# Last head pair of a FoX/RWKV-7 layer: its third block turned by VectorE and transfers, its fourth by TensorE

## The chip, the core and the metric

The kernel runs on one core of one Trainium2 chip. The core has TensorE (PE, matrix multiply, results in PSUM), VectorE (DVE), ScalarE (ACT), GpSimd (POOL) and SyncE (SP), whose queue issues nearly all transfers of this kernel; 16 DMA engines carry them. The metric is device time in microseconds (us) of one execution, as a median of several.

## The reference, cut to what matters

One layer for 256 frames and a width of 4096, all in float32. An input projection makes the columns of 16 attention heads (q, k, v of 128 columns each), of 32 RWKV-7 heads (r, k, v of 64 columns each) and of a gate z. Attention and RWKV results are gated by silu(z), joined, projected by `w_out`, and normalised with the residual.

```python
proj = jnp.einsum('bsd,dc->bsc', x, w_in)
fox_out = _fox_attention(fq, fk, fv, log_f)            # 16 heads of 128
y = _rwkv7_scan(rh, decay, kh, vh, -kk, kk * ah)       # 32 heads of 64
...
h = jnp.concatenate([fox_out, rwkv_out], axis=-1) * jax.nn.silu(z.astype(f32))
out = jnp.einsum('bsc,cd->bsd', h.astype(x.dtype), w_out)
x = _layernorm(ALPHA * x.astype(f32) + out.astype(f32), ln_gain, ln_bias, LN_EPS)
```

## The kernel before

**Tiling.** The projection is done in 8 pairs (`n` = 0 to 7, `G // 2` of them) of 4 blocks (`b` = 0 to 3) of 512 columns each. A block is 16 weight pieces `q` of 512 KB; each piece is split by ACT and DVE into a high and a low part (`w_qh`, `w_ql`; lines 141 and 142), and three matmuls per step (lines 147 to 149) give nearly float32 precision. After the 8 pairs comes the output projection over 8 blocks of 512 columns, with pieces `wo_q` and the same split (lines 882 to 884).

**Order of the work.** PE runs the projection's matmuls without a break, and everything else is done beside them. `block` calls `slot()` after every six matmuls (one k for both halves of the frames, or two k for one half), 32 times a block; in the first two blocks of the output projection (pieces 0 to 13) there is one slot per k. At a slot each generator in `sides` is advanced to its next `yield`; `wait(n)` is n slots. So slots fix the order in which instructions are written down. A planner in the framework then orders each engine's instructions by the time at which it reckons that their inputs are ready, so an instruction may move ahead of earlier written ones; `issue` (line 281) pins a transfer behind the one written before it on SP's queue. On the chip each engine and SP's queue work through the order they were given, and wait where an input is late.

**The blocks of a pair.** Block 0 holds RWKV r and k, block 1 RWKV v and attention v, block 2 the columns q, k, z of attention head 2n and z of RWKV (`fq`, `fk`, `zf`, `zr`), block 3 the same for head 2n+1. The results have frames on partitions; attention and gate want columns on partitions, so blocks 0, 2 and 3 are turned by `unload` (line 798), which starts two slots (`LAG`) after its block's end; block 2's waits in addition until the RWKV work of the pair before is done.

There are two ways to turn a block. In the general one (lines 809 to 815 and 843 to 847) DVE transposes both halves of `bk` in 32 x 32 squares (line 811), two slots later `turn` writes them in four transfers of 128 KB to a DRAM tile `bt`, two per slot, and four more transfers of 128 KB read `fq`, `fk`, `zf` and `zr` back from it in the wanted order, in rows of 32 elements. In the other (lines 832 to 841) PE transposes eight 128 x 128 tiles of `bk` against the identity `ident` into two PSUM tiles `tr`, and ACT copies them out. `last` (line 806) decides: in the kernel before, blocks 2 and 3 of pair 7 go by PE and all others by DVE and transfers.

**After the turn.** ACT scales `fq` (line 848), `fox(i, ...)` is started as a side (line 849), and the gate's tanh and product follow (`silu2`, line 367). `fox` multiplies q and k after 4 slots (`fsp`, lines 745 and 746), forms the softmax on DVE and ACT (lines 751 to 755), transposes it on DVE (line 757), copies it to `pT` (line 761), and multiplies it with v (`fop`, lines 766 and 767) 12 slots after `fsp`. `gate` (line 373) forms `h` and its two parts `hl`, and three slots later stores them in DRAM (`hd`, line 386) where the index k is under 29. Head 14 has k = 28 and is stored; head 15 (k = 30) and the RWKV halves 29 and 31 go straight into their tiles. `unload` of block 3 waits until `fox` of head 14 is through (line 828).

**What runs at the same time.** In block 3 of pair 7 the tiles of x come free step by step, and `get_h` (line 854) loads the stored `hd` of 256 KB each into them, 29 loads for the output projection, on SP's queue between the weight loads (line 218). RWKV of pair 7 solves its triangular systems on DVE meanwhile (lines 601 and 604), writes the result to `td` and reads it back as `T` (lines 611 and 613), turns v by transfers (`vt`, `vv`), and ends in the first blocks of the output projection. Weight loads have four buffers, the high parts four and the low parts three.

Of the kernel before, what the change touches and what calls it, by code (L numbers as in the profile page):

```python
# [21 lines left out]
G = 16  # L22
# [62 lines left out]
def layer(ctx: ExitStack, tc: tile.TileContext, xt, xtok, w_main, w_lora, w_first, muv, w_o, up, par, mulora, fbias, lng, lnb, cst, out):  # L85
# [9 lines left out]
    def pst(name):  # L95
        return ps.tile([P, 512], F32, tag="ps", name=name)
# [93 lines left out]
    def wait(n):  # L190
        for _ in range(n):
            yield

    def side(gen):
        sides.append(gen)
# [72 lines left out]
    def t256(tag, name, bufs=1):  # L268
        return rp.tile([P, S], F32, tag=tag, name=name, bufs=bufs)
# [10 lines left out]
    def issue(out, src):  # L280
        tc.keep_in_program_order(nc.sync.dma_start(out=out, in_=src))

    def turn(src, name, each=2):
        _, m, cols = src.shape
        d = dram.tile([cols // B, B, m, 4, B], F32, tag=f"dt{m}_{cols}", name=name, bufs=2)
        s = src.rearrange("p m (q t) -> p m q t", t=B)
        for a in range(4):
            issue(d[:, :, :, a, :].rearrange("q i m t -> i m q t"), s[B * a : B * (a + 1)])
            if a % each == each - 1:
                yield  # L290
        return d

    def shifted(p, n, i):
        r = t256(f"s{n}", f"s{n}_{i}", 2)
        lerp(p, prm[:, 7 + n, i : i + 1], omm[:, n, i : i + 1], r)
        return r
# [70 lines left out]
    def silu2(z, key):  # L367
        th = t256("zt", key + "t")
        nc.scalar.activation(th, z, AF.Tanh, scale=0.5)
        nc.vector.scalar_tensor_tensor(z, th, 1.0, z, ALU.add, ALU.mult)  # L370
        szs[key] = z
# [419 lines left out]
    def turned_back(d):  # L791
        return d.rearrange("(u b) i m a t -> u (b i) (m a t)", b=4).rearrange("u p s -> p u s")
# [5 lines left out]
    def unload(n, b, bk, vt):  # L798
        yield from wait(LAG)
        if b == 0:  # L800
            while n and 2 * n - 1 not in prepared:
                yield
        elif b == 2:
            while n and n - 1 not in done:
                yield
        last = n == G // 2 - 1 and b > 1
        if b == 3 and not last:
            yield from wait(BEHIND)
        if not last:
            for m in range(2):  # L810
                nc.vector.transpose(bk[:, m, :], bk[:, m, :])
            yield from wait(2)
            d = yield from turn(bk, f"bt{n}_{b}")
            unloading.clear()
            yield
        if b == 0:
            for u in range(2):
                i = 2 * n + u
                while n and n - 1 not in bonned:
                    yield  # L820
                raw = rp.tile([P, 2, S], F32, tag="s2", name=f"raw{i}")
                issue(raw, turned_back(d[8 * u : 8 * u + 8]))
                yield from wait(LAND)
                for j in range(2):
                    rk[i, j] = shifted(raw[:, j, :], j, i)
            return
        i = 2 * n + b - 2
        while i and i - 1 not in foxed:
            yield
        fq, fk = t256("fq", f"fq{i}"), t256("fk", f"fk{i}")  # L830
        zf, zr = t256("szf", f"zf{i}"), t256("szr", f"zr{i}", 2)
        if last:
            for h, pair in enumerate(((fq, fk), (zf, zr))):
                tr = pst(f"tr{h}")
                for t in range(2):
                    for m in range(2):
                        nc.tensor.transpose(tr[:, t * S + m * P : t * S + (m + 1) * P], bk[:, m, (2 * h + t) * P : (2 * h + t + 1) * P], ident)
                for t in range(2):
                    nc.scalar.copy(pair[t], tr[:, t * S : (t + 1) * S])
                yield  # L840
            unloading.clear()
        else:
            for j, t in enumerate((fq, fk, zf, zr)):
                issue(t, d[4 * j : 4 * j + 4].rearrange("b i m a t -> (b i) (m a t)"))
                if j % 2:
                    yield
            yield from wait(LAND - 1)
        nc.scalar.mul(fq, fq, FOX_SCALE)
        side(fox(i, fq, fk, vt))
        yield  # L850
        silu2(zf, f"f{i}")
        silu2(zr, f"r{i}")
# [62 lines left out]
    for n in range(G // 2):  # L915
        for b in range(4):
            acc = block(n, b)
            while unloading or b == 2 and n not in turned:
                slot()
            bk = rp.tile([P, 2, OB], F32, tag="bk", name=f"bk{n}_{b}") if n or b else bk_0  # L920
            for m in range(2):
                if b == 1:
                    nc.scalar.copy(bk[:, m, : 2 * P], acc[m][:, : 2 * P])
                elif not n and not b:
                    nc.scalar.copy(bk[:, m, P:], acc[m][:, :LB])
                else:
                    nc.scalar.copy(bk[:, m, :], acc[m])
            if b == 0:
                muvs[n] = rp.tile([P, 2 * P], F32, tag="prod", name=f"muv{n}")
                nc.sync.dma_start(out=muvs[n], in_=muv[n : n + 1, :].to_broadcast([P, 2 * P]))  # L930
            if b == 1:
                vd = vds[n % 2]
                bks[n] = bk[:, :, : 2 * P]
                nc.sync.dma_start(out=vd[1:].rearrange("(m p) c -> p m c", m=2), in_=bk[:, :, : 2 * P])
                vs_[n] = rp.tile([P, 2, 2 * P], F32, tag="vs", name=f"vs{n}")
                nc.sync.dma_start(out=vs_[n], in_=vd[:S].rearrange("(m p) c -> p m c", m=2))
                while n and 2 * n - 1 not in foxed:
                    slot()
                vt = rp.tile([P, 2, 2 * P], F32, tag="vt", name=f"vt{n}")
                for m in range(2):  # L940
                    nc.scalar.copy(vt[:, m, :], acc[m][:, 2 * P :])
            if b != 1:
                unloading.append(n)
                side(unload(n, b, bk, vt))
# [57 lines left out]
    def moments(m):  # L1002
        mv = rpool.tile([P, 2], F32, name=f"mv{m}")
        sd = rpool.tile([P, 1], F32, name=f"sd{m}")
        rs = rpool.tile([P, 1], F32, name=f"rs{m}")
        s2 = rpool.tile([P, 1], F32, name=f"s2{m}")
        zh = rpool.tile([P, 1], F32R, name=f"zh{m}")
        z = factors(m, "d")
        nc.gpsimd.memset(z[:, 3:5], 1.0)
        za = factors(m, "a") if m else None  # L1010
        add(m, NB - 1)
        nc.vector.bn_aggr(mv, sums if m else st[m].rearrange("p b s -> p (b s)"))
        mean = mv[:, 0:1]
        nc.scalar.activation(sd, mv[:, 1:2], AF.Sqrt, bias=lneps)
        nc.vector.reciprocal(rs, sd)
        nc.vector.tensor_tensor(s2, mean, rs, ALU.mult)
        nc.vector.tensor_copy(zh, s2)
        nc.vector.tensor_copy(z[:, 0:3:2], zh.bitcast(F32).to_broadcast([P, 2]))
        last = nc.vector.tensor_tensor(z[:, 1:2], s2, zh.bitcast(F32), ALU.subtract)
        s2s.append(s2)  # L1020
        if m:
            for n, (v, at) in enumerate(((mean, (slice(0, 3, 2), slice(1, 2))), (sd, (slice(3, 5), slice(5, 6))))):
                h = rpool.tile([P, 1], F32R, name=f"zah{n}")
                nc.scalar.copy(h, v)
                nc.scalar.copy(za[:, at[0]], h.bitcast(F32).to_broadcast([P, 2]))
                nc.scalar.activation(za[:, at[1]], h.bitcast(F32), AF.Identity, scale=-1.0, bias=v)
        rss.append(rs)
        return z, za, last.ins
# [18 lines left out]
    z0, _, last = moments(0)  # L1047
# [18 lines left out]
    z1, za, last = moments(1)  # L1066
# [7 lines left out]
    for n in range(HALVED):  # L1074
        b = HALVED + n
# [62 lines left out]
```

## Time and profile before

| | us |
|---|---|
| median of 3 runs | 1917.26 (1916.16 to 1917.36) |
| the profiled execution's own time | 1917.13 |
| its span in the profile | 1915.3 |
| PE busy | 1903.0 (99%) |
| PEld (weight loads into PE) busy | 1584.8 (83%) |
| DVE busy | 1398.3 (73%) |
| ACT busy | 985.9 (51%) |
| POOL busy | 261.5 (14%) |

1917.13 - 1915.3 = 1.8 us of the execution lie outside the span. Times below are in us from the span's start. "PE" rows are matmuls; a matmul's length overlaps that of its neighbours, so their pace is read from start to start. The DMA column of a table by windows is the mean busy share of the 16 DMA engines. The granted TensorE clock is 0.999 of full speed.

### The profile page before, as it was taken

Reading aid. Unit: us, or ns where it says so; the run is one execution under the profiler, and the core shown is the slowest. Engines: PE = TensorE matmul, PEld = TensorE weight load, DVE = VectorE, ACT = ScalarE, POOL = GpSimd, SP = SyncE. Lnnn points to the kernel's source line nnn. Section 1 sums busy time; section 2 is a strip of 40 time slices with the busy share of each in tenths; the row PEclk is TensorE's granted clock in tenths of the full one; section 3 lists DMA queues with packets and bytes.
Section 4 is the critical chain, followed back from the end, with each engine's and each line's share of the span. In section 5 each row is a group of like instructions: output and inputs, shape, how many; then the busy total and the mean of one; then the engine's idle time right before and its main releaser. Section 6 shows DMA issues by size and latency. Waiting matters only on the chain.

```text
span 1915.3 us, 27998 instructions
## 1 busy us (share of the span) xinstructions
PE 1903.0 (99%) x9784; PEld 1584.8 (83%) x9784; DVE 1398.3 (73%) x2359; ACT 985.9 (51%) x1543; POOL 261.5 (14%) x463
## 2 busy tenths in 40 slices
PE   9999999999999999999999999999999999999998
PEld 9878888888888888888888888888888878888886
DVE  6677868786877687768776877787778865765555
ACT  6554565455545654465446554645464554444332
POOL 0022102110211021102200220022002201000000
PEclk9999999999999999999999999999999999999999
DMA  9578767876787677767876687668767976876664
GB/s 338 152 232 230 205 198 235 229 216 190 228 232 220 189 228 224 230 191 217 233 227 193 208 242 226 194 208 246 215 196 207 300 255 199 271 222 202 183 203 170
DMA packets 269682, 420.58 MB, mean 220 GB/s; under 512 B 142370, under 2 KB 169396, under 8 KB 269540
## 3 DMA queue, kind: packets, MB, share of 16 engines
q1 hardware_dynamic: 269108, 418.10, 72.8%
q8 instruction: 77, 1.26, 0.3%
q10 hardware_dynamic: 432, 0.69, 0.1%
q14 instruction: 65, 0.53, 0.1%
HBM read 389.07 MB, written 29.64 MB: 219 GB/s over the span
## 4 chain that ended last, share of the span: by engine, by line
PE 97%; DVE 1%; ACT 0%; issue 0%; DMA 0%; DVEq 0%; ACTq 0%
PE acc L147 24%; PE acc L149 24%; PE acc L148 24%; PE oacc L884 6%; PE oacc L882 6%; PE oacc L883 6%; PE rh L648 1%; PE gp L534 1%; PE up L679 1%; PE sp L689 1%; PE accl L147 1%; PE accl L148 1%; PE accl L149 1%; PE yp L711 0%; PE yp L709 0%; PE fsp L746 0%
## 5 line engine op out<-in xcount | busy, mean ns | idle before, releaser
L761 POOL COPY pT<-lg 32x96 f32<-32x96 f32 x128 | 58.5, 457 | 641.7 <-DVE lg L757 636.9
L604 DVE TENSOR_REDUCE xc<-prod 128x8 f32<-128x16 f32 (+30 forms) x248 | 72.7, 293 | 6.5
L571 POOL COPY BKt<-BK 32x192 f32<-32x192 f32 x128 | 68.6, 536 | 58.6 <-DVE BK L568 53.6
L601 DVE TENSOR_TENSOR prod<-Nb,xc 128x8 f32<-128x8 f32 (+30 forms) x248 | 72.2, 291 | 3.0
L142 DVE TENSOR_TENSOR w_0l<-w,w_0h 128x1024 fp32r<-128x1024 f32 x31 | 38.7, 1248 | 38.2 <-ACT w_0h L141 25.0
L141 ACT CAST w_0h<-w 128x1024 fp32r<-128x1024 f32 x31 | 32.5, 1048 | 51.5 <-DMA w<-in_w_main_dram 31.0
L142 DVE TENSOR_TENSOR w_11l<-w,w_11h 128x1024 fp32r<-128x1024 f32 x31 | 37.9, 1224 | 23.3 <-PE acc L149 17.7
L142 DVE TENSOR_TENSOR w_9l<-w,w_9h 128x1024 fp32r<-128x1024 f32 x31 | 38.0, 1225 | 21.6 <-issue 8.0
L142 DVE TENSOR_TENSOR w_10l<-w,w_10h 128x1024 fp32r<-128x1024 f32 x31 | 38.0, 1224 | 20.6 <-ACT w_10h L141 8.0
L142 DVE TENSOR_TENSOR w_15l<-w,w_15h 128x1024 fp32r<-128x1024 f32 x31 | 38.0, 1226 | 19.4 <-issue 15.9
L141 ACT CAST w_8h<-w 128x1024 fp32r<-128x1024 f32 x31 | 32.6, 1052 | 37.6 <-DMA w<-in_w_main_dram 12.5
L141 ACT CAST w_1h<-w 128x1024 fp32r<-128x1024 f32 x31 | 32.7, 1054 | 34.8 <-DMA w<-in_w_main_dram 18.9
L142 DVE TENSOR_TENSOR w_6l<-w,w_6h 128x1024 fp32r<-128x1024 f32 x31 | 37.9, 1221 | 17.3 <-ACT hry L722 10.3
L147 PE MATMUL acc<-w_15h,x 128*128 128x512 f32 x124 | 50.2, 405 | 0.0
L147 PE MATMUL acc<-w_9h,x 128*128 128x512 f32 x124 | 50.0, 403 | 0.0
L141 ACT CAST w_6h<-w 128x1024 fp32r<-128x1024 f32 x31 | 32.6, 1053 | 33.0 <-PE acc L148 23.0
L147 PE MATMUL acc<-w_14h,x 128*128 128x512 f32 x124 | 49.5, 399 | 0.0
L141 ACT CAST w_13h<-w 128x1024 fp32r<-128x1024 f32 x31 | 32.5, 1050 | 32.6 <-PE acc L148 31.9
L147 PE MATMUL acc<-w_1h,x 128*128 128x512 f32 x124 | 49.1, 396 | 0.0
L147 PE MATMUL acc<-w_2h,x 128*128 128x512 f32 x124 | 49.1, 396 | 0.0
L147 PE MATMUL acc<-w_0h,x 128*128 128x512 f32 x124 | 49.1, 396 | 0.0
L147 PE MATMUL acc<-w_5h,x 128*128 128x512 f32 x124 | 49.1, 396 | 0.0
(818 smaller groups left out, 6633.7 us busy)
## 6 DMA issues: line engine op xcount, KB each, us to landing
w<-in_w_main_dram SPq DMA_DIRECT2D x496, 512.0 KB, 4.1
wo<-in_w_o_dram SPq DMA_DIRECT2D x128, 512.0 KB, 4.1
bt<-bk SPq DMA_DIRECT2D x88, 128.0 KB, 4.2
Nb<-nd SPq DMA_DIRECT2D x16, 512.0 KB, 4.6
hd<-hl SPq DMA_DIRECT2D x29, 256.0 KB, 2.2
h<-hd SPq DMA_DIRECT2D x29, 256.0 KB, 6.1
wr<-in_w_first_dram SPq DMA_DIRECT2D x15, 384.0 KB, 6.1
lr<-in_w_lora_dram SPq DMA_DIRECT2D x14, 336.0 KB, 6.5
```

The lines of the kernel that those rows point to most:

```text
L141: nc.scalar.copy(hi[:, :n], src[:, :n])
L142: latest[0] = nc.vector.tensor_tensor(lo[:, :n], src[:, :n], hi[:, :n].bitcast(F32), ALU.subtract)
L147: nc.tensor.matmul(acc[:, :n], xs[k][:, 0, tt], hi[:, o : o + n], start=(k == 0), stop=False)
L148: nc.tensor.matmul(acc[:, :n], xs[k][:, 1, tt], hi[:, o : o + n], start=False, stop=False)
L149: nc.tensor.matmul(acc[:, :n], xs[k][:, 0, tt], lo[:, o : o + n], start=False, stop=(k == KT - 1))
L571: nc.gpsimd.tensor_copy(BKt[B * b : B * (b + 1), :, :, B * a : B * (a + 1)], BK[B * a : B * (a + 1), :, : NCH - 1, B * b : B * (b + 1)])
L601: first = nc.vector.tensor_tensor(prod[:, :, :, s + 1 :], nb[:, :, s : s + 1, s + 1 :].to_broadcast([P, 2, NJ, w]), xc[:, :, :, s + 1 :], ...
L604: solved = nc.vector.tensor_reduce(xc[:, :, :, s : s + 1], prod[:, :, :, s:], AX.X, ALU.add)
L761: (nc.gpsimd.tensor_copy if b % 2 else nc.scalar.copy)(pT[B * b : B * (b + 1), :, B * a : B * (a + 1)], lg[B * a : B * (a + 1), :, B * b : ...
L882: nc.tensor.matmul(acc, ht[k][:, 0, tt], hi, start=(k == 0), stop=False)
L883: nc.tensor.matmul(acc, ht[k][:, 1, tt], hi, start=False, stop=False)
L884: nc.tensor.matmul(acc, ht[k][:, 0, tt], lo, start=False, stop=(k == KT - 1))
```

## The change

One condition changes. Block 2 of pair 7 no longer meets `last`, so it takes the general way: two DVE transposes, four transfers to DRAM, four back. Block 3 of pair 7 keeps the PE transposes.

```diff
--- before.py
+++ after.py
@@ -803,7 +803,7 @@
         elif b == 2:
             while n and n - 1 not in done:
                 yield
-        last = n == G // 2 - 1 and b > 1
+        last = n == G // 2 - 1 and b == 3
         if b == 3 and not last:
             yield from wait(BEHIND)
         if not last:
```

## The prediction

> **What bounds the kernel now.** I read the page's first part, then the chain that ended last, then PE's waits in the stretch that the change touches (1490 to 1620 us), then that stretch in the chain.
>
> ```profile
> PE 1903.0 (99%) x9784; PEld 1584.8 (83%) x9784; DVE 1398.3 (73%) x2359; ACT 985.9 (51%) x1543; POOL 261.5 (14%) x463
> ...
> PE 97%; DVE 1%; ACT 0%; issue 0%; DMA 0%; DVEq 0%; ACTq 0%
> ```
>
> ```profile
> PE sp L689 <- DVE UV L682: 0.3, 1, 0.3
> ```
>
> PE is the chain: 97% of the span hangs on it, and between 1490 and 1620 us it waits once, for 0.3 us. So whatever leaves PE shortens the run by its own length, and whatever is added elsewhere costs nothing until it makes PE wait. The question is how far each side chain is from doing that.
>
> ```profile
> 1497.32 0.44 PE tr L837 x4
> ...
> 1499.15 0.44 PE tr L837 x4
> ...
> 1524.78 0.43 PE fop L766 x2
> ...
> 1560.59 1.22 DVE wo_7l L142
> 1561.85 0.73 PE oacc L884 x2
> ```
>
> The last two rows are a warning. At 1560.59 the chain leaves PE for DVE: the low part of weight piece wo_7 is ready at 1560.59 + 1.22 = 1561.81, and the matmuls that need it start at 1561.85. Here the weights have no lead left. Further up they have one:
>
> ```profile
> 1516.71 1.23 DVE L142 TENSOR_TENSOR w_10l<-w,w_10h 128x1024 fp32r<-128x1024 f32 x1
> ```
>
> ```profile
> 1522.35 0.39 PE L149 MATMUL acc<-w_10l,x 128*128 128x512 f32 x1
> ```
>
> w_10l is ready at 1517.94 and first used at 1522.35: a lead of 4.4 us. Between these two places it drains. What drains it is the transfer traffic of this stretch, in a table by windows of 6 us (PE, PEld, DVE, ACT, POOL busy, clock, DMA share, GB/s); the first two rows are the same place in pair 6, where block 2 is already turned by transfers:
>
> ```profile
> 1308.00:1314.00 6.00, 6.00 (x28) 4.99 (x27) 5.74 (x17) 2.11 (x2) 0.00 (x0) 1.00 0.78 163
> 1314.00:1320.00 6.00, 6.00 (x28) 4.95 (x28) 4.28 (x11) 2.42 (x3) 0.00 (x0) 1.00 0.91 217
> ...
> 1498.00:1504.00 6.00, 6.00 (x30) 4.93 (x30) 4.41 (x12) 4.04 (x9) 0.00 (x0) 1.00 1.02 374
> 1504.00:1510.00 6.00, 6.00 (x29) 5.03 (x28) 5.00 (x14) 2.13 (x3) 0.00 (x0) 1.00 0.89 225
> 1510.00:1516.00 6.00, 6.00 (x28) 4.96 (x27) 5.81 (x18) 3.14 (x7) 0.04 (x1) 1.00 0.96 285
> 1516.00:1522.00 6.00, 6.00 (x28) 4.98 (x27) 5.76 (x14) 4.98 (x13) 3.35 (x8) 1.00 0.98 355
> 1522.00:1528.00 6.00, 6.00 (x29) 5.01 (x28) 5.75 (x13) 2.59 (x4) 0.00 (x0) 1.00 0.97 363
> 1528.00:1534.00 6.00, 6.00 (x28) 4.96 (x27) 5.62 (x12) 2.11 (x2) 0.00 (x0) 1.00 0.79 254
> 1534.00:1540.00 6.00, 6.00 (x28) 4.99 (x27) 4.95 (x9) 2.54 (x4) 0.00 (x0) 1.00 0.99 374
> 1540.00:1546.00 6.00, 6.00 (x32) 4.95 (x32) 4.41 (x10) 4.34 (x10) 0.00 (x0) 1.00 0.65 172
> 1546.00:1552.00 6.00, 6.00 (x28) 4.99 (x27) 1.99 (x3) 2.47 (x4) 0.00 (x0) 1.00 0.92 320
> ```
>
> In pair 7 the DMA engines are near full from 1498 on, because the 29 loads of `hd` run beside the weights. No earlier pair has that, so pair 6 proves only half: that the general way fits into this place with free DMA engines.
>
> **The change part by part.**
>
> PE loses two groups of four transposes: 2 x 0.44 = 0.88 us on the path, a sure gain. The Trainium skill, "VectorE: DVE Perf Modes", section Rules for kernel authors, speaks against the change: a 128 x 128 transpose belongs on TensorE where a PSUM result will do. Its table (The three transpose paths) gives 390 ns for one, in bf16; eight would be an estimated 3.1 us of PE, and the sum below would come out 2.2 us lower. The chain's 0.44 us for four decides.
>
> ```profile
> L839 ACT COPY fq<-tr x2: 373/373/373, 1497.8 to 1542.3; 128x256 f32<-128x256 f32 x2
> ```
>
> ```profile
> L811 DVE STREAM_TRANSPOSE bk<-bk x44: 667/702/714, 74.9 to 1404.6; 128x512 f32<-128x512 f32 x44
> ```
>
> ACT loses four copies of about 0.37 us, 1.5 us that were on no path. DVE gains two transposes, 1.40 us. They come right after the block's end; the windows from 1498 to 1510 leave DVE 1.59 + 1.00 = 2.6 us idle, which covers them. If that cover were gone they would sit ahead of the weight splits, and 1.40 us would come off a lead of 4.4. I take zero.
>
> SP's queue gains eight transfers, and the head's later work moves. By the slots, `fox` of head 14 starts 7 slots later: two from DVE's transposes to the first write, two for the writes, one to the reads, two for the reads and two of `wait(LAND - 1)`, in place of two slots of PE transposes. Here is how that looks in pair 6, and the same marks of the two pairs to carry it over:
>
> ```profile
> 1285.51 3.79 SPq L554 DMA_DIRECT2D nd<-gb  x8
> ...
> 1309.04 3.78 SPq L281 DMA_DIRECT2D bt<-bk  x4
> ...
> 1315.42 0.33 SPq L281 DMA_DIRECT2D fq<-bt  x1
> ```
>
> ```profile
> 1361.08 0.43 SPq L281 DMA_DIRECT2D hd<-hl  x1
> ```
>
> ```profile
> 1475.18 4.00 SPq L554 DMA_DIRECT2D nd<-gb  x8
> ...
> 1523.45 0.33 SPq L218 DMA_DIRECT2D wo<-in_w_o_dram  x1
> 1527.84 0.32 SPq L281 DMA_DIRECT2D hd<-hl  x1
> ```
>
> ```profile
> L766 PE MATMUL fop<-pT,vt x2: 377/378/378, 1343.5 to 1343.7; 128*128 128x256 f32 x2
> ```
>
> The pairs lie 1475.18 - 1285.51 = 189.7 us apart. So in the changed kernel the writes should start near 1498.7, the reads near 1505.1, `fop` of head 14 should go from 1524.78 to about 1533.2, and its store `hd` from 1527.84 to about 1550.8 (in pair 6 it stands behind the RWKV transfers). `foxed` of head 14 comes 3 slots before block 3's `unload` asks for it (12 + 16 + 3 = slot 31 of block 3, against slot 34), so head 15 is not written down later. Between 1309.04 + 3.78 and 1315.42 the queue also turns v and loads a weight piece; the reads wait for the writes to land, and a weight load written behind them waits too. On the other side the old store held the queue idle from 1523.8 to 1527.8, and that hold goes. Both are put at zero by themselves: what they do to the weights is in the next term.
>
> The DMA engines gain 8 x 128 KB = 1.05 MB in runs of 128 bytes. No row prices it alone. In pair 6 the windows 1308 to 1320 were busy for (0.78 + 0.91) x 6 = 10.1 us and moved (163 + 217) x 6 = 2280 KB; at the full rate of window 1534 to 1540 (374 GB/s at 0.99, so 378) these take 6.0 us. The excess of 4.1 us belongs to the short runs of `bt` (1.05 MB) and `vt` (three of 64 KB in that stretch, 0.2 MB), so 3.4 us to `bt`; with its bytes (1.05 MB / 378 GB/s = 2.8) it takes **6.2 us** of all 16 engines. The Trainium skill, "DMA: Bandwidth & Descriptors", section Specifications, asks for 512 bytes or more a transfer for the full rate; it gives no time for less, and by bytes alone the term would be 2.8 us. Pair 6's excess says that it is more.
>
> The nine windows from 1498 to 1552 leave 0 + 0.66 + 0.24 + 0.12 + 0.18 + 1.26 + 0.06 + 2.10 + 0.48 = 5.1 us of DMA time free. If all of it can be used, the weights are 6.2 - 5.1 = 1.1 us late where they have no lead; if none, 6.2 us. I leave out the 2.1 us of 1540 to 1546, where the queue is busy issuing the small `T` reads and can't start loads earlier, and count the rest: 6.2 - 3.0 = **3.2 us late, which PE waits** between about 1545 and 1575. What was late there is then early: the traffic after 1576 is lighter, and RWKV's results have time to spare.
>
> The sum is made against the profiled execution's 1917.13: - 0.88 + 3.2 gives 1919.45. The median stands 0.13 higher, so I add that: **1919.6 us**.
>
> **The rivals.**
>
> *Hidden.* The free DMA time suffices, since the queue no longer idles before the store, and the loads of `hd` start earlier and spread better. For it: no pair before waits on PE at this place; against it: wo_7's missing lead. Time: 1917.26 - 0.88 = 1916.4; with the 0.3 us wait gone as well, 1916.1. It decides where no weight row shows PE waiting.
>
> *In-order wait, the slower side.* ACT works in a fixed order, and the tanh of `zf` now stands in it behind a transfer, with the weight casts queued behind it.
>
> ```profile
> 1320.20 0.42 ACT L369 ACTIVATE f12t<-zf 128x256 f32<-128x256 f32 x1 [0.97 <-DMA zf<-bt]
> ```
>
> ```profile
> fq<-bt SPq DMA_DIRECT2D x1, 128.0 KB, 3.3
> ```
>
> ```profile
> h<-hd SPq DMA_DIRECT2D x29, 256.0 KB, 6.1
> ...
> nb<-ncd SPq DMA_DIRECT2D x1, 128.0 KB, 8.7
> ```
>
> In pair 6 ACT already waits 0.97 us there, with 3.3 us from issue to landing. In pair 7's traffic transfers take 6.1 (`hd`) to 8.7 us (`nb`), so the wait grows by 2.8 to 5.4 us, to 3.8 to 6.4. The splits' lead of 4.4, less the 3.2 us of lateness above, leaves 1.2 us; beyond that PE waits, for 2.6 to 5.2 us in block 3 itself, on top of the 3.2. Time: 1917.26 - 0.88 + 3.2 + 2.6 to 5.2 = 1922.2 to 1924.8, and 1927.8 with the DMA term at its upper bound. It decides once ACT waits over 1.2 us for `zf` of head 14. Against it: the planner may put the tanh behind more casts, and PE's order with it.
>
> *RWKV late.* In pair 6 the solve ends later than in pair 7, and its place in the changed kernel may move by some microseconds. I give this no chance of its own: its results `hl` are early.
>
> ```profile
> 1613.79 0.42 DVE L382 TENSOR_TENSOR hl<-h,hl 128x256 fp32r<-128x256 f32 x1
> ```
>
> ```profile
> L882 PE MATMUL oacc<-wo_14h,hl x4: 389/389/389, 1629.7 to 1635.9; 128*128 128x512 f32 x4
> ```
>
> The last part is written at 1614.2, and no `hl` is used before 1629.7.
>
> **How the numbers follow.** Forecast (weights 1.1 to 6.2 us late, 1917.5 to 1922.6 us): 0.38. Hidden: 0.25. In-order wait: 0.34. Something that gains more than PE's transposes, for which I see no row: 0.03. About 0.2% is what a measurement of this kernel can tell from no change, 3.8 us here, so the border to slower is 1921.1. The in-order wait lies above it, and the forecast's upper part with 0.05: slower 0.39. Faster by as much has only the 0.03. The rest, 0.58, is within. The range runs from the hidden case with the runs' spread, 1915.8, to the in-order wait short of its worst, 1927.
>
> **What would show it.** Right: `tr` only near 1541; transposes of `bk` near 1497, writes near 1499, reads near 1505; DMA shares near 1.0 from 1498 to 1540; PE waits of some 3 us in all for `wo_` parts between 1545 and 1575, and PE busy 0.9 us less. The hidden case shows no PE wait over 0.4 us, the in-order wait a row of ACT held over 2 us by `zf` or `fq`, and PE waiting for `w_` parts before 1537. A wait of PE on `fsp` or `fop` of head 14, or on RWKV's results after 1600, would refute my reading of the order.

## The result, and the profile after

| | before | after |
|---|---|---|
| median of 22 runs each, us | 1917.32 (1916.15 to 1921.62) | 1921.95 (1918.73 to 1924.7) |
| ratio | | 1.0024, 95% interval 1.0018 to 1.003 |
| span of the profiled execution, us | 1915.3 | 1920.7 |

The kernel became slower by 0.24%, 4.6 us, although PE has less to do. The first part of the page of the changed kernel, and the line of shares from its chain that ended last:

```profile
PE 1904.8 (99%) x9776; PEld 1582.7 (82%) x9776; DVE 1399.7 (73%) x2361; ACT 985.4 (51%) x1539; POOL 262.8 (14%) x463
...
PE 94%; DVE 2%; DMA 2%; ACT 1%; issue 1%; SPq 0%; DVEq 0%; ACTq 0%
```

PE has eight matmuls fewer (9784 before), yet its busy time rose by 1.8 us (a stretch at half clock, told in the last section, is part of it), and its share of the chain fell from 97% to 94%: now it waits. PE's waits between 1490 and 1620 us in the changed kernel (what PE wanted, for whom it waited, us in total, times, longest):

```profile
PE oacc L882 <- ACT wo_5h L141: 1.5, 1, 1.5
PE fop L766 <- POOL pT L761: 1.1, 1, 1.1
...
PE oacc L884 <- DVE wo_3l L142: 0.2, 1, 0.2
```

There are two places: head 14's `fop` in block 3, and the pieces wo_3 to wo_5 of the output projection. What the removed transposes leave can be seen from the tile `tr`, which is now used for block 3 only:

```profile
L837 PE MATMUL tr<-cs,bk x8: 270/272/277, 1540.4 to 1544.4; 128*128 128x128 f32 x8
```

Next, SP's queue of the changed kernel over time (start, us, instruction; "..." leaves rows out):

```profile
1497.77 5.05 SPq L281 DMA_DIRECT2D bt<-bk  x4
1502.92 0.66 SPq L281 DMA_DIRECT2D vt<-UV  x1
1503.68 0.81 SPq L218 DMA_DIRECT2D w<-in_w_main_dram  x1
1505.61 0.33 SPq L281 DMA_DIRECT2D fq<-bt  x1
...
1537.60 0.38 SPq L857 DMA_DIRECT2D h<-hd  x1
1543.95 0.80 SPq L611 DMA_DIRECT2D td<-xc  x2
...
1545.32 0.38 SPq L218 DMA_DIRECT2D wo<-in_w_o_dram  x1
1545.80 3.79 SPq L613 DMA_DIRECT2D T<-td  x8
1549.69 0.38 SPq L281 DMA_DIRECT2D hd<-hl  x1
...
1551.17 0.35 SPq L218 DMA_DIRECT2D wo<-in_w_o_dram  x1
```

The same places of the queue in the kernel before:

```profile
1500.50 0.40 SPq L218 DMA_DIRECT2D w<-in_w_main_dram  x1
...
1538.53 0.80 SPq L611 DMA_DIRECT2D td<-xc  x2
...
1540.21 0.39 SPq L218 DMA_DIRECT2D wo<-in_w_o_dram  x1
...
1545.68 0.38 SPq L218 DMA_DIRECT2D wo<-in_w_o_dram  x1
```

The four writes of `bt` take the queue 5.05 us to issue, and the load of w_8, next but one behind them, goes out at 1503.68 in place of 1500.50. Forty microseconds later comes the second hold: from 1537.98 to 1543.95 the queue stands still with `td` at its head. The queue also stood there in the kernel before, for 4.5 us, but `td` went out at 1538.53. `td` waits for RWKV's solve on DVE, which now ends 5.4 us later, and the loads of wo_4 and wo_5 (1545.32 and 1551.17, before 1540.21 and 1545.68) stand behind it. ACT's side of both holds (in brackets: idle time before the instruction, and who ended it):

```profile
1508.54 1.05 ACT L141 CAST w_8h<-w 128x1024 fp32r<-128x1024 f32 x1 [4.50 <-DMA w<-in_w_main_dram]
...
1510.66 0.42 ACT L369 ACTIVATE f14t<-zf 128x256 f32<-128x256 f32 x1 [0.75 <-DMA zf<-bt]
```

```profile
1556.88 0.36 ACT L643 COPY Q<-qt 32x256 f32<-32x256 f32 x1 [3.85 <-DMA h<-hd]
1557.27 1.04 ACT L141 CAST wo_5h<-wo 128x1024 fp32r<-128x1024 f32 x1
```

ACT stood 4.50 us for the load of w_8. Behind that cast in its fixed order are head 14's steps and the next casts, and DVE waits for them in the middle of the solve, as its subtractions `w_ql` show (changed kernel, then the same piece before):

```profile
1509.62 1.23 DVE L142 TENSOR_TENSOR w_8l<-w,w_8h 128x1024 fp32r<-128x1024 f32 x1 [1.36 <-ACT w_8h L141]
...
1530.70 1.23 DVE L142 TENSOR_TENSOR w_13l<-w,w_13h 128x1024 fp32r<-128x1024 f32 x1 [2.39 <-ACT w_13h L141]
```

```profile
1511.61 1.22 DVE L142 TENSOR_TENSOR w_8l<-w,w_8h 128x1024 fp32r<-128x1024 f32 x1
```

With w_9l and w_11l there are four such waits, 6.8 us together, and none before these four in the kernel before. So the first hold made the solve late, and the late solve made the second hold; the experiments test this. The table by windows of 6 us of the changed kernel (columns as in the prediction) shows in its last two, the share and GB/s, that the DMA engines were not short of time in the second hold:

```profile
1534.00:1540.00 6.00, 6.00 (x28) 4.92 (x27) 5.76 (x13) 1.98 (x3) 0.00 (x0) 1.00 1.03 393
1540.00:1546.00 6.00, 6.00 (x33) 4.87 (x31) 4.44 (x10) 3.88 (x9) 0.00 (x0) 1.00 0.40 136
```

They moved 136 GB/s while the loads that PE was about to need waited in the queue.

### The profile page after: what moved, and what is told of

It reads as the page before. It is cut to its first block, busy times and chain, and to the rows that moved or that the text cites. A ratio compares the mean times of both kernels' runs of the same rounds, so it can differ in the third digit from the quotient of the medians.

```text
span 1920.7 us, 27994 instructions
## 1 busy us (share of the span) xinstructions
PE 1904.8 (99%) x9776; PEld 1582.7 (82%) x9776; DVE 1399.7 (73%) x2361; ACT 985.4 (51%) x1539; POOL 262.8 (14%) x463
## 4 chain that ended last, share of the span: by engine, by line
PE 94%; DVE 2%; DMA 2%; ACT 1%; issue 1%; SPq 0%; DVEq 0%; ACTq 0%
PE acc L147 23%; PE acc L149 23%; PE acc L148 23%; PE oacc L884 6%; PE oacc L882 6%; PE oacc L883 6%; PE rh L648 1%; PE gp L534 1%; DMA w<-in_w_main_dram 1%; PE up L679 1%; PE sp L689 1%; PE accl L149 1%; PE accl L147 1%; PE accl L148 0%; PE yp L711 0%
## 5 line engine op out<-in xcount | busy, mean ns | idle before, releaser
L460 POOL COPY hr<-hr 32x16 f32<-32x16 f32 x64 | 46.1, 720 | 23.6 <-DVE hr L457 21.2
L147 PE MATMUL acc<-w_11h,x 128*128 128x512 f32 x124 | 49.1, 396 | 0.0
L147 PE MATMUL acc<-w_6h,x 128*128 128x512 f32 x124 | 49.1, 396 | 0.0
```

Of the source, the lines that this page charges most:

```text
L147: nc.tensor.matmul(acc[:, :n], xs[k][:, 0, tt], hi[:, o : o + n], start=(k == 0), stop=False)
```

## The experiments

All are compared with the kernel before on the same chip. The figure that places the loss is the shift: the start of the first matmul of a weight piece, minus that of the kernel before, both counted from the first matmul of w_13 in block 2 (1484.92 us before, 1483.98 after), so that differences at the start of an execution fall out. In us, from one profiled execution each; w_5 and w_13 belong to block 3, "end" is wo_13 of the first output block, and later pieces keep that shift. At w_5, -0.9 are the removed transposes and the rest is head 14's `fsp`, which comes later. In the same way a piece that now stands ahead of head 14's `fop`, and not behind it, comes about 0.7 earlier (e1_delay_only at w_13). From wo_5 on, a stretch at half clock (last section) is part of the shift in the changed kernel, e5, e7 and e8, and twice in e3.

```text
kernel               w_5    w_13   wo_0   wo_5   wo_7   end    median us (ratio, 95%)
changed kernel      -1.40  +0.92  +1.51  +4.47  +6.24  +5.93   1921.95 (1.0024, 1.0018 to 1.003)
e1_delay_only       -0.46  -0.68  +0.01  +0.01   0.00   0.00   1916.94 (0.9997, 0.9988 to 1.0007)
e2_transfers_only   +0.01  +0.27  +0.50  +3.77  +4.41  +3.97   1921.72 (1.0021, 1.0011 to 1.003)
e3_td_behind        -1.40  -0.40  +0.10  +0.11  +6.74  +7.18   1922.92 (1.0028, 1.0016 to 1.004)
e4_bt_pool          -1.40  -1.62  -0.93  +0.88  +1.06  +0.99   1918.47 (1.0004, 0.9994 to 1.0013)
e5_q_dve            -1.40  -0.01  +0.49  +2.84  +5.12  +4.39   1920.95 (1.0014, 1.0005 to 1.0023)
e6_pool_q_dve       -1.40  -1.62  -0.94  -0.94  +0.16  -0.33   1917.87 (0.9997, 0.9989 to 1.0006)
e7_writes_pool      -1.40  -1.33  -0.65  +0.96  +2.60  +2.64   1918.56 (1.0002, 0.9993 to 1.0011)
e8_reads_pool       -1.40  +0.50  +1.03  +3.99  +6.50  +6.50   1921.40 (1.0016, 1.0007 to 1.0025)
e9_cast_first       -1.40  -1.62  -0.94  +0.07  +1.93  +2.82   1920.96 (1.0011, 1.0002 to 1.002)
e10_writes_spaced   -1.40  -1.61  -1.61  +1.20  +1.39  +2.29   1919.35 (1.001, 1.0001 to 1.0019)
e11_casts_first     -1.40  -0.69  +1.98  +4.96  +5.91  +7.03   1922.72 (1.003, 1.0018 to 1.0041)
```

**Is it that head 14 comes later?** The kernel before, with head 14 only put off by seven slots:

```diff
+        if last and b == 2:
+            yield from wait(7)
         nc.scalar.mul(fq, fq, FOX_SCALE)
```

> The kernel before, block 2 of pair 7 still turned by PE, but head 14's work written down 7 slots later, where the change puts it. Theory Queue (SP's queue works in order: the bt transfers hold the weight loads behind them, the splits come late, the solve ends late, and td at the queue's head then holds wo_4 and wo_5): no transfers, so nothing is held: 1917 to 1918.5 us, td issued within 2 us of where it was (1538.5). Theory Bytes (the 16 DMA engines are full and 1.05 MB more makes weights late): no bytes added, 1917 to 1918. Theory Move (head 14's later work alone spoils the order on ACT, DVE and SP): 1920 to 1922.

It measured 1916.94 us, no different from before, with no wait of PE but the old 0.3 us. The later place of head 14 costs nothing by itself.

**Is it the transfers?** The kernel before, PE transposes and all, with the eight transfers added; nobody reads what they bring.

```diff
+    def extra(bk):
+        yield from wait(1)
+        d = yield from turn(bk, "bt_extra")
+        yield
+        for j, (tag, bufs) in enumerate((("am", 1), ("ae", 1), ("eI", 1), ("t", 5))):
+            t = rp.tile([P, S], F32, tag=tag, name=f"ex{j}", bufs=bufs)
+            issue(t, d[4 * j : 4 * j + 4].rearrange("b i m a t -> (b i) (m a t)"))
+            if j % 2:
+                yield
...
+        if last and b == 2:
+            side(extra(bk))
```

> The kernel before with PE transposes and head 14 in its old place, plus the eight bt transfers at the slots where the change has them, from bk as it stands and back into free tiles that nobody reads (this is added work; the output does not depend on it). Queue: the cast of w_8 waits for its load as after (some 4.5 us), PE waits, 1920 to 1923 us. Bytes: much the same time, 1920 to 1923, but with ACT's waits spread over all weight casts and DMA share near 1.0 throughout. Move: 1917 to 1918.

It measured 1921.72 us: the transfers alone, with nothing depending on them, cost as much as the whole change. The sign expected at w_8 didn't come: the planner had put head 14's exponentials ahead of the cast of w_7h, and ACT waited 6.12 us for their input from DVE, not for a load. So this trace can't tell the queue from the bytes. In its queue and in PE's waits the second hold is there again:

```profile
1543.16 0.80 SPq L611 DMA_DIRECT2D td<-xc  x2
```

```profile
PE oacc L894 <- ACT wo_5h L141: 1.5, 1, 1.5
```

**Their bytes, or their place in the queue?** The changed kernel with the same eight transfers issued by GpSimd (`turn` and `issue` hand `queue` on to the transfer):

```diff
+        queue = nc.gpsimd if n == G // 2 - 1 and b == 2 else nc.sync
...
-            d = yield from turn(bk, f"bt{n}_{b}")
+            d = yield from turn(bk, f"bt{n}_{b}", queue=queue)
...
-                issue(t, d[4 * j : 4 * j + 4].rearrange("b i m a t -> (b i) (m a t)"))
+                issue(t, d[4 * j : 4 * j + 4].rearrange("b i m a t -> (b i) (m a t)"), queue)
```

> The changed kernel with the eight bt transfers of pair 7's block 2 issued from POOL's queue, not SP's. Queue: weight loads pass, the cast of w_8 waits under 1 us for its load, fop of head 14 isn't late, td is issued by 1541, 1916.5 to 1918.5 us. Bytes: the same bytes at the same time, 1920.5 to 1922. Move: 1920.5 to 1922.

It measured 1918.47 us. In its trace POOL issues the four writes, and the DMA engines move the same bytes at a high share (windows of 6 us):

```profile
1497.69 3.45 POOL L281 DMA_DIRECT2D bt<-bk  x4 [5.99 <-DVE xc L604]
```

```profile
1498.00:1504.00 6.00, 6.00 (x28) 4.96 (x27) 5.23 (x13) 2.35 (x3) 3.14 (x4) 1.00 1.02 327
1504.00:1510.00 6.00, 6.00 (x28) 4.97 (x27) 4.79 (x13) 2.11 (x2) 2.19 (x4) 1.00 1.01 243
```

The shift stays at -0.93 up to wo_0: the first stall is gone, so the bytes don't cause it, and the place on SP's queue is what is left; the planner's order on ACT moved as well, which a later kernel tests. One wait of 1.5 us for wo_5h is left.

**Can the second hold be mended by order?** The changed kernel with `td` of pair 7 put behind the loads of wo_4 and wo_5 (`loads` keeps each load's instruction):

```diff
+        held = 0
+        while n == G // 2 - 1 and "wo0_5" not in loads:
+            held += 1
+            yield
...
-            nc.sync.dma_start(out=td[u].rearrange("q c (g j) s -> (q c g) (j s)", g=NG), in_=flat(xc[:, u]))
+            with tc.issue_after(loads["wo0_5"].ins) if held else ExitStack():
+                nc.sync.dma_start(out=td[u].rearrange("q c (g j) s -> (q c g) (j s)", g=NG), in_=flat(xc[:, u]))
...
-        yield from wait(W["d2"] - 1)
+        yield from wait(W["d2"] - 1 - held)
```

> The changed kernel with one order changed on SP's queue: td of pair 7 stands behind the loads of wo_4 and wo_5, not before them. Queue: the cast of wo_5 is no longer late, the PE wait of 1.5 us before wo_5 and the slow clock after it go, about 4.5 us of the loss: 1917 to 1918.5 us; the wait of fop of head 14 stays. Bytes: the same bytes in nearly the same stretch, 1920.5 to 1922. Move: as after, 1920.5 to 1922.

1922.92 us, above the ranges of all three theories; the expected gain didn't come. wo_5 was in time (shift +0.11), but now `T` at the head of the queue waited for `td`, which landed behind the loads, and wo_6 and wo_7 came late in place of wo_4 and wo_5 (SP's queue, then PE's waits):

```profile
1550.35 3.81 SPq L620 DMA_DIRECT2D T<-td  x8
1554.27 0.37 SPq L219 DMA_DIRECT2D wo<-in_w_o_dram  x1
```

```profile
PE oacc L889 <- ACT wo_7h L141: 2.1, 1, 2.1
PE oacc L889 <- ACT wo_6h L141: 1.5, 1, 1.5
```

So the hold moved and did not go. Half clock came twice here, so the shift at the end is not the hold's alone.

**Writes or reads?** Two kernels with only the four writes, or only the four reads, on GpSimd's queue; the diff is that of e4_bt_pool with `queue` in one of its two places.

> The changed kernel with only the four writes of block 3 on GpSimd's queue, the four reads on SyncE's. Theory Writes hold the queue: the load of w_8 is issued at about 1500.5 as in the kernel before, no wait at w_8 to w_14, td at about 1539, time as with all eight moved, 1918.5 (1917.7 to 1919.3). Theory Reads hold the queue: td stays later than 1542 and the time is 1921 or more.

> The changed kernel with only the four reads of block 3 on GpSimd's queue, the four writes on SyncE's; order of the other engines all but unchanged. Theory Writes hold the queue: w_8 is issued at about 1503.7 as in the changed kernel, td near 1543, time 1921 to 1922.5. Theory Reads hold the queue: td at about 1539 and 1918 to 1919.

With the writes moved it measured 1918.56 us, with the reads moved 1921.40. In e7_writes_pool the load of w_8 goes out early and ACT casts it without waiting for it:

```profile
1499.73 0.33 SPq L218 DMA_DIRECT2D w<-in_w_main_dram  x1
```

```profile
1506.23 1.06 ACT L141 CAST w_8h<-w 128x1024 fp32r<-128x1024 f32 x1 [1.66 <-PE acc L148]
```

That points to the writes, though `td` went out at 1540.68, not at about 1539 as expected. The other half of the pair is weaker evidence: in e8_reads_pool the planner put head 14's scaling ahead of the cast of w_8, and ACT waited there 7.36 us for `fq`, so two holds are mixed in it.

```profile
1511.55 0.42 ACT L849 ACTIVATE fq<-fq 128x256 f32<-128x256 f32 x1 [7.36 <-DMA fq<-bt]
```

**The four in a row, or 5 us of queue at all?** The changed kernel, all transfers on SP, with two slots between the writes:

```diff
-    def turn(src, name, each=2):
+    def turn(src, name, each=2, pause=0):
...
+            yield from wait(pause if a < 3 else 0)
...
-            d = yield from turn(bk, f"bt{n}_{b}")
+            d = yield from turn(bk, f"bt{n}_{b}", pause=2 if n == G // 2 - 1 and b == 2 else 0)
```

> The changed kernel, all eight transfers on SyncE as there, but two steps of the loop lie between the four writes of block 3, so that the loads of w_8, w_9 and w_10 are issued between them. Theory Held queue: what costs is that four writes stand in a row ahead of the weight loads; w_8 is issued before 1502, no wait at w_8 to w_14, and the time is about that with the writes on GpSimd's queue, 1918.6 (1917.5 to 1919.8). Theory Amount: SyncE's queue has 5 us more to issue, wherever it stands: td stays later than 1542 and the time is 1921 or more.

1919.35 us; the first stall is gone (shift -1.61 at wo_0). In its queue the loads of w_8 to w_10 stand between the writes:

```profile
1498.70 1.37 SPq L281 DMA_DIRECT2D bt<-bk  x2
...
1502.32 0.56 SPq L218 DMA_DIRECT2D w<-in_w_main_dram  x1
...
1504.22 0.70 SPq L281 DMA_DIRECT2D bt<-bk  x1
1505.02 1.12 SPq L218 DMA_DIRECT2D w<-in_w_main_dram  x1
...
1507.02 0.63 SPq L281 DMA_DIRECT2D bt<-bk  x1
```

Part of the expectation missed: w_8 went out at 1502.32, not before 1502.

Over all traces, counted from the first matmul of w_13 in block 2, late loads of w_8 and a late `td` go together. With the four writes in a row on SP's queue (changed kernel, e2, e5, e8, e11) w_8's load goes out 3.0 to 4.4 us later than before, and `td` 4.9 to 7.2. With the writes on GpSimd's queue (e4, e6, e7, e9) the load goes out 0.4 us earlier and `td` 1.0 to 2.6 later; with the writes spaced it is 1.8 and 2.7.

**ACT's order instead?** In the kernels without the first stall the planner had also put the casts of w_9 and w_10 ahead of head 14's steps on ACT, which is what the prediction's in-order rival would have cured. So this kernel keeps the changed kernel's queue and changes only that order:

```diff
+        behind = "w7_3_10" if n == G // 2 - 1 and b == 2 else None
+        while behind and behind not in casts:
+            yield
+        with tc.issue_after(casts[behind].ins) if behind else ExitStack():
+            nc.scalar.mul(fq, fq, FOX_SCALE)
...
+        with tc.issue_after(casts["w7_3_10"].ins) if key in ("f14", "r14") else ExitStack():
+            nc.scalar.activation(th, z, AF.Tanh, scale=0.5)
```

> The changed kernel with SyncE's transfers in the same order up to the store of head 14, but on ScalarE the scaling of fq and the two tanh of head 14 stand behind the cast of w_10h, as they do where the writes went to GpSimd's queue or were spaced. Theory Held queue: w_8 is still issued near 1503.7, ScalarE still waits over 3 us for its load, td comes later than 1542, and the time is 1920.5 to 1922.5. Theory ScalarE order (the in-order wait of the prediction): the casts no longer stand behind head 14's transfers, no PE wait before 1537, td near 1540, 1918.6 (1917.6 to 1919.6), as with the writes on GpSimd's queue.

1922.72 us, just above the 1920.5 to 1922.5 of the held queue and far from the 1918.6 of ACT's order. The casts stand first and still wait, for their loads:

```profile
1508.55 1.05 ACT L142 CAST w_8h<-w 128x1024 fp32r<-128x1024 f32 x1 [4.82 <-DMA w<-in_w_main_dram]
1513.30 1.05 ACT L142 CAST w_9h<-w 128x1024 fp32r<-128x1024 f32 x1 [3.70 <-DMA w<-in_w_main_dram]
```

The ACT-order theory falls for the first stall. Together with e10_writes_spaced this settles its cause: the four writes in a row ahead of the weight loads, on the one in-order queue.

**What is left at wo_5 and wo_7.** In the changed kernel and in e4_bt_pool ACT copies `Q` from `qt` ahead of the cast of wo_5h, and the copy waits for PE: the row at 1556.88 above names a load of `h`, but PE's last matmul of `qt` starts only at 1556.40. Two kernels, from the changed one and from e4_bt_pool, give that copy of the last pair to DVE:

```diff
-            (nc.vector.tensor_copy if j else nc.scalar.copy)(Q[b].rearrange("p u c s -> p (u c s)"), qp[b, : 2 * P])
+            (nc.vector.tensor_copy if j or n == G // 2 - 1 else nc.scalar.copy)(Q[b].rearrange("p u c s -> p (u c s)"), qp[b, : 2 * P])
```

> The changed kernel with one edit: in the last pair the first of the two copies Q<-qt goes to VectorE too, so that the cast of wo_5h no longer stands behind it on ScalarE. Theory ScalarE order: the wait of 1.5 us for wo_5h goes, and with it the half clock behind it (1.6 us): 1921.95 - 3.1 = 1918.8 (1918 to 1919.8), no wait for wo_5h and no window under 0.9 of the clock between 1555 and 1570. Theory Loads only: the load of wo_5 (issued 1551.2) or those behind it end last anyway; the wait shows at wo_5h, wo_6h or wo_7h as before, within 0.7 of 1921.95.

> The kernel with the eight transfers of block 3 on GpSimd's queue, and both copies Q<-qt of the last pair on VectorE. If queue and ScalarE order are the two causes, both are gone and the transposes' 0.9 us remain as gain: 1918.47 - 1.5 = 1917.0, and 1916.4 if nothing else is left; ratio 0.9990 to 1.0000. If the transfers' bytes cost by themselves, a wait for a wo part stays in the trace and the time is over 1918.

The first measured 1920.95 us and met neither expectation: against the kernel before on its own chip it loses 3.0 us, where the changed kernel loses 4.6, and the intervals of the two ratios overlap. Its cast of wo_5h, no longer behind the copy, waits for its load:

```profile
1555.49 1.04 ACT L141 CAST wo_5h<-wo 128x1024 fp32r<-128x1024 f32 x1 [3.63 <-DMA wo<-in_w_o_dram]
```

With the transfers off SP's queue as well, e6_pool_q_dve measured 1917.87 us, as fast as before and no faster. The transposes' 0.94 us are still there at wo_5 (-0.94) and are lost at wo_7, where a new wait has come up:

```profile
PE oacc L883 <- ACT wo_7h L141: 1.1, 1, 1.1
```

There the cast of wo_7h stood behind head 15's exponentials on ACT. The last kernel, built on e6_pool_q_dve, puts the cast ahead of them, and the subtraction wo_7l ahead of head 15's reciprocals on DVE:

```diff
+        tail = "wo0_7" if i == NF - 1 else None
+        while tail and tail not in casts:
+            yield
...
+            with tc.issue_after(casts[tail].ins) if tail else ExitStack():
+                nc.scalar.activation(lg[:, blk, :], lg[:, blk, :], AF.Exp, bias=st[:, m : m + 1], accum_out=st[:, 2 + m : 3 + m])
+            with tc.issue_after(los[tail].ins) if tail else ExitStack():
+                nc.vector.reciprocal(st[:, 4 + m : 5 + m], st[:, 2 + m : 3 + m])
```

> The kernel with the eight transfers on GpSimd's queue and both copies Q<-qt on VectorE, and now also the cast of wo_7h on ScalarE ahead of head 15's two exponentials, and the subtraction wo_7l on VectorE ahead of its reciprocals. Theory: what was left (a wait of 1.1 us for wo_7h) is again an order on ScalarE; without it the transposes' gain stays: 1917.87 - 1.1 = 1916.8, ratio 0.999 to 0.9997, no wait over 0.5 us between 1490 and 1620. Rival: the load of wo_7 or the late head 15 sets the place; a wait of about 1 us shows elsewhere and the time stays within 0.4 of 1917.9.

1920.96 us, no better, and outside both expected ranges. The cast now waits 3.95 us for its load, as the rival expected, and head 15 is later for nothing:

```profile
1562.24 1.04 ACT L143 CAST wo_7h<-wo 128x1024 fp32r<-128x1024 f32 x1 [3.95 <-DMA wo<-in_w_o_dram]
```

The load itself also went out later here (1554.63, against 1550.31 in e6_pool_q_dve), so this kernel alone doesn't show what held the cast in e6_pool_q_dve. That trace does: the last update of the load's semaphore comes at 1558.53 and the cast starts at 1558.62, so the load had no lead there either, whoever stood ahead of the cast. The start of this load is held too. SP waits, before issuing it, until the load of wo_5 has landed: that is at 1551.10 before, 1555.96 in the changed kernel and 1550.23 in e6_pool_q_dve, and wo_7's load follows at 1551.18, 1556.02 and 1550.31. So a late wo_5 hands its lateness on to wo_7. No version tried here beats the kernel before by more than the measurement can tell.

## Why the prediction came near, for a wrong cause

It named 1919.6 us within 1915.8 to 1927; the median is 1921.95, inside the range but just beyond its own border of 1921.1 for slower, so its likeliest class, no change, was not met. That the time came this near is luck: a lateness of about the right size was put down to the wrong cause. By its own steps:

- **PE loses 0.88 us.** Right: between w_1 and w_3 of block 3, where they stood, the changed kernel gains 0.94 us on the one before.
- **The places.** Right for the writes (1498.7 named, 1497.77 seen), the reads (1505.1, 1505.61) and the store `hd` (1550.8, 1549.69). Wrong for `fop` of head 14: 1533.2 named, 1529.93 seen, because the planner put it before a moment at which `pT` was ready. PE waits 1.1 us for it, which the prediction had called a refutation of its reading of the order, and in this it is.
- **"Both are put at zero by themselves."** This is the step that failed. It had the hold of SP's queue in hand, the 3.78 us that pair 6's four writes took and a weight load behind them, set the old store's hold of 4 us against it, and passed both on to the DMA engines' time. The old hold did go, but the runs put the loss on the new one: 5.05 us of issue with w_8 behind it, gone with the writes on another queue (1918.47 and 1918.56) and mostly gone with the writes spaced on the same one (1919.35).
- **DMA engines: 6.2 us wanted, 3.0 us free, so 3.2 us late.** Lateness came at the pieces named, wo_3 to wo_5, but as waits of 1.9 us in all and up to 1.7 us of half clock, and not for this reason: in e4_bt_pool the same bytes ran with shares of 1.02 and 1.01 and the first stall was away. What the bytes cost by themselves at wo_7 no run separates. Leaving out 1540 to 1546 because the queue can't start loads then was right, and should have been the main thread: that stretch, with a share of 0.40, is where the loads waited.
- **In-order wait.** Its time (1922.2 to 1924.8) begins 0.25 us above the median, and part of its effect is seen (casts held on ACT, then `wo_` parts late; PE waits for no `w_` part before 1537). But its cause is not: ACT waited 0.75 us for `zf`, under the 1.2 us from which it was to decide, and 4.50 us for the load of w_8. e11_casts_first took the order away and nothing came back.
- **RWKV late, no chance.** Wrong reason for a wrong zero. It looked at what needs RWKV's results, after 1614, and not at what stands behind RWKV's own transfer in the queue: a solve that ends 5.4 us later holds `td`, and `td` holds wo_4 and wo_5.
- **Hidden.** Falls: the loss is 4.6 us. And e6_pool_q_dve shows how little there was to gain: even with both holds mended, the 0.94 us end at wo_7, the place that the prediction had marked as without lead.

## What to carry to other kernels

On a queue that issues in order, price a transfer by how long its issue holds the queue and by what stands right behind it, ahead of any sum of bytes; with four scattered writes in a row this kernel lost 4.6 us, with loads between them 1.5, and with the writes on another queue 0.6. A step that makes a side computation late is paid where that computation's own transfer reaches the head of the queue, so look there and not only at the users of its result. And a gain on the busiest engine is worth no more than the lead of the next load on its way: 0.9 us saved at 1500 were waited away at 1560.

## What the runs showed of the hardware

**PE's clock halves after a short pause, sometimes.** The pause before wo_5h costs more than itself. Windows of 1 us of the changed kernel (PE busy, PEld, DVE, ACT, POOL, granted clock, DMA share, GB/s):

```profile
1558.00:1559.00 1.00, 0.63 (x2) 0.30 (x2) 0.65 (x1) 0.31 (x1) 0.00 (x0) 0.81 0.82 296
1559.00:1560.00 1.00, 0.75 (x2) 0.37 (x2) 0.57 (x1) 0.64 (x1) 0.00 (x0) 0.50 0.30 89
1560.00:1561.00 1.00, 1.00 (x3) 0.79 (x3) 0.56 (x1) 0.41 (x1) 0.00 (x0) 0.50 0.37 119
1561.00:1562.00 1.00, 1.00 (x4) 0.73 (x3) 0.67 (x1) 0.00 (x0) 0.29 (x1) 0.50 0.88 344
1562.00:1563.00 1.00, 1.00 (x6) 0.82 (x5) 0.52 (x2) 0.00 (x0) 0.29 (x1) 0.98 1.05 420
```

The clock is at one half for 0.38 + 3 + 0.04 = 3.42 us, and in it matmuls follow each other every 0.43 us. By an estimate from these figures that takes up to 3.42 / 2 = 1.7 us, and PE's busy time grew by about as much with less work:

```profile
1560.65 0.63 PE L883 MATMUL oacc<-wo_5h,h 128*128 128x512 f32 x1
1561.08 0.63 PE L884 MATMUL oacc<-wo_5l,h 128*128 128x512 f32 x1
```

In e7_writes_pool, after a wait of 1.5 us at the same place, the half clock lasts 3.42 us again, by the same sum. Of the eight kernels whose trace has a PE wait of 1.5 us for a piece wo_5 to wo_7, the clock fell in four (the changed kernel, e3, e7, e8) and stayed full in four (e2, e4, e9, e11). It fell in e5 too, where the waits were 1.0 and 0.5 us. This is e2_transfers_only, a microsecond after its wait:

```profile
1559.00:1560.00 1.00, 0.47 (x3) 0.37 (x3) 1.00 (x2) 0.45 (x1) 0.25 (x1) 1.00 0.48 170
```

The Trainium skill, "TensorE: Matmul & The Clock Gate", section Part 1: The HAM clock gate (the "warmup" mystery), has the clock fall to half after an idle window of about 3.4 us whose start runs freely of the kernel. The length of 3.42 us agrees, and a window that runs freely would fit the two outcomes after one and the same pause, which no run here tests. The pause that sufficed here, 1.53 us ahead of wo_5h, is under half of such a window; here the measurement decides. Whether this also makes the spread of single runs, 1918.73 to 1924.7 us, was not tried.

**Of four scattered writes in a row, the later ones hold the queue.** In the changed kernel three of the four writes of `bt` took SP's queue 0.60 to 0.67 us each, and the third 2.99 (least, median and most in ns):

```profile
L281 SPq DMA_DIRECT2D bt<-bk x4: 600/664/2987, 1497.8 to 1502.2; - x4
```

In the 22 earlier groups of four of that execution the first write always took 0.57 to 0.70 us and the third 0.71 to 2.31. With other transfers behind the second and the third (e10_writes_spaced) all four took 0.60 to 0.72. In e3_td_behind, with the same writes in the same place, the third took 1.61, so the size of the first stall changes from one execution to the next. What the queue waits for in the third write the traces don't show.
